# Two causal convolutions: reading the products from PSUM instead of from SBUF copies

## The chip, the cores and the metric

One core of a Trainium2 chip runs the whole program. The time is the device time of one execution in microseconds (us); the number compared is the median of several executions of the same kernel. TensorE (PE) does the matmuls and writes into PSUM, a small memory of banks; VectorE (DVE), ScalarE (ACT) and GpSimd (POOL) do the elementwise work; SyncE (SP) issues most DMA transfers between HBM and SBUF.

## The reference

One step of a hybrid decoder layer over 2048 prompt rows and 8 sequences of 8 sample rows, 1024 columns wide, all in float32. A projection of the normalised rows feeds three mixers (gated delta rule, S5, HGRN2); their outputs are concatenated and projected back; then comes a channel mixer with a convolution, and a gated embedding. Two places hold a causal convolution of each column over time, with 4 taps for q, k and v and with 3 taps for the up projection:

```
def causal_dwconv(x, buf, w):
    xp = jnp.concatenate([buf.astype(x.dtype), x], axis=1)
    y = xp[:, 0:t] * w[0]
    for j in range(1, width):
        y = y + xp[:, j:j + t] * w[j]
    return y, xp[:, t:]
...
z = rmsnorm(h, norm_mix[i]) @ w_in[i]
qkv, buf_qkv = causal_dwconv(z_qkv, conv_qkv[i], dn_conv_w[i])
...
h = h + jnp.concatenate([o_a, o_b, o_c], axis=-1) @ w_out[i]
up, buf_ffn = causal_dwconv(rmsnorm(h, norm_ffn[i]) @ ffn_w_up[i], conv_ffn[i], ffn_conv_w[i])
a_ff, b_ff = jnp.split(up, 2, axis=-1)
h = h + (jax.nn.silu(a_ff) * b_ff) @ ffn_w_down[i]
```

The prompt starts with zero rows before it; each of the 8 sample sequences starts with given state rows (`state_conv_qkv`, `state_conv_ffn`). The last rows before the end are outputs too.

## The kernel before

The rows are cut into four groups of 512; the last has the 64 sample rows with it. The matmuls are float32 products in three passes (high by high, low by high, high by low part), so a unit of 128 output columns by up to 512 rows takes 24 matmuls into one of three PSUM banks named `mm`. Stages follow one another: phase 1 (input projection, to about 900 us), the first output projection for groups 0 and 1 (phase 3, about 900 to 1090), their up projection (phase 4, to 1784), the second output projection for groups 2 and 3 (1784 to 1891), their up projection (to 2416), the down projection (phase 5, to 2934), and the end (phase 6). All that is the foreground; its matmuls are called `mm`.

Beside it runs the background: generators for the three mixers, for norms and for setup, whose matmuls go into PSUM banks named `mx`. Each chunk of the delta rule needs a triangular inverse, made four times in the program by 31 pairs of TENSOR_TENSOR `R<-Q,R` and TENSOR_REDUCE `R<-R` on VectorE. HGRN2 goes group by group, each in two halves: loads into `hw`, levels that multiply and merge (`mx<-hw`), the merged tile `mx<-ident,hw`, four rounds on the state `SH`, a norm, a transpose `mx<-ident,b`, and a store to `oT`.

The order of everything is decided while the program is built. `Pace` (L44) keeps for each engine the time at which a cost model sees it free, from every instruction issued, its operands and the rings of its tiles. After each foreground matmul `tick` (L740) runs evacuations that are due (`later`, L754: when the model sees the tile ready, or after so many ticks at the latest) and then lets background generators take steps whose inputs the model sees ready. `need` (L749) is the exception: where the foreground cannot go on without a flag, it runs the background alone, forced, until the flag is set. On the chip each engine then simply takes its instructions in that order. All instructions are issued from one helper, `call` at L71, so rows of the profile are told apart by their tiles.

A convolution unit goes like this. `conv_evac` (L885) lets ACT copy the product from its bank into an SBUF tile `raw` with room for the rows before it, and write the last tap, `y = w * product`; the bank is then free. `edges` fills the rows before (on POOL, from `tail`, `ftail`, `stq` or `fst`), `conv` (L894) adds the other taps on VectorE with SCALAR_TENSOR_TENSOR `y<-raw,w,y`, and `keep` lets POOL save the last rows. The ring `raw` has two tiles of 603 columns. It has two other users: `ffn_state` (L2255) loads the 11 blocks of 16 state rows of the second convolution into it (`fs_rows`), transposes them on TensorE and copies them to `fst`; and in the first output projection every fourth pair of residual tiles stands in it (`pair`, L2184). Other residual pairs are `h1x` tiles of the ring `nx` (four tiles of 1024 columns, shared with the norms) or `y` tiles.

Of the kernel before, what the change touches and what calls it, by code (L numbers as in the profile page):

```python
# [9 lines left out]
F32 = mybir.dt.float32  # L10
# [4 lines left out]
OP = mybir.AluOpType  # L15
# [431 lines left out]
class Model:  # L447
# [420 lines left out]
    def edges(self, raw, taps, first, tail, rows):  # L868


        nc = self.nc
        k = taps - 1
        if first:
            nc.gpsimd.memset(raw[:, 0:k], 0.0)
        else:
            nc.gpsimd.tensor_copy(raw[:, 0:k], tail)
        if rows is not None:
            nc.gpsimd.tensor_copy(self.sample_part(raw, taps)[:, :, 0:k], rows)

    @staticmethod  # L880
    def sample_part(raw, taps):
        k = taps - 1
        return raw[:, k + 512:k + 512 + NSEQ * (k + ST)].rearrange("p (s t) -> p s t", t=k + ST)

    def conv_evac(self, raw, y, ps, c1, m, taps, w):  # L885

        k = taps - 1
# [6 lines left out]
    def conv(self, y, raw, w, taps, n):  # L894

        for j in range(taps - 1):
            self.nc.vector.scalar_tensor_tensor(y[:, :512], raw[:, j:j + 512], w[:, j:j + 1], y[:, :512], op0=OP.mult,
                                                op1=OP.add)
        if n > 512:
            ys, rs = y[:, 512:].rearrange("p (s t) -> p s t", t=8), self.sample_part(raw, taps)  # L900
            for j in range(taps - 1):
                self.nc.vector.scalar_tensor_tensor(ys, rs[:, :, j:j + 8], w[:, j:j + 1], ys, op0=OP.mult, op1=OP.add)

    def keep(self, raw, taps, last, tail, out):

        nc = self.nc
        k = taps - 1
        if last:
            nc.gpsimd.tensor_copy(out[:, 0:k], raw[:, 512:512 + k])
            nc.gpsimd.tensor_copy(out[:, k:].rearrange("p (s t) -> p s t", t=k), self.sample_part(raw, taps)[:, :, 8:])  # L910
        else:
            nc.gpsimd.tensor_copy(tail, raw[:, 512:512 + k])

    def p1_evac(self, g, kind, b, c1, m, ps):
        nc = self.nc
        n = self.group(g)[1]
        if c1 == 0:
            self.y = self.cv.tile([128, 512 + NS], F32, tag="y", name="y", bufs=3)
            if kind == "qkv":
                self.raw = self.cv.tile([128, 3 + 512 + NSEQ * 11], F32, tag="raw", name="raw")  # L920
                self.edges(self.raw, 4, g == 0, self.tail[:, b],
                           self.stq[:, b].rearrange("p (s t) -> p s t", t=3) if g == 3 else None)
        y = self.y
        if kind == "qkv":
            self.conv_evac(self.raw, y, ps, c1, m, 4, self.cw[:, b])
# [14 lines left out]
    def p1_finish(self, g, kind, b, y):  # L940
# [15 lines left out]
        def conv(raw=self.raw if kind == "qkv" else None):  # L956
            self.conv(y, raw, self.cw[:, b], 4, n)
            self.keep(raw, 4, g == 3, self.tail[:, b], self.cso[:, b])
            self.later(y, silu, 9)

# [10 lines left out]
        if kind == "qkv":  # L971
            self.later(self.raw, conv, 12)
        else:
            self.later(y, bound if kind == "hf" else out, 12)
# [1198 lines left out]
    def phase3(self, units, wo, between, direct):  # L2173
# [4 lines left out]
        half_tile = lambda tag, w, bufs: self.cv.tile([128, w], F32, tag=tag, name="xh", bufs=bufs)[:, :512]  # L2178
        y_tile = lambda: half_tile("y", 512 + NS, 3)
# [675 lines left out]
```

## Time and profile before

| | |
|---|---|
| median of 3 runs | 3197.21 us (3195.34 to 3198.12) |
| the profiled execution | 3197.67 us, its span 3195.9 us |
| mean granted TensorE clock | 0.981 of full speed |
| TensorE busy | 3059.7 us, 96% of the span |
| VectorE, ScalarE, GpSimd busy | 1882.4, 1196.0 and 899.9 us |

A share of busy time is an average over all stages. A row of a timeline gives the start, the duration, the engine and the instruction, and in brackets how long its engine had stood idle before it and what released it. Tile numbers are left out, so `mm` is any of the three product banks.

### The profile page before, as it was taken

The numbers are of one execution on the slowest core, as the hardware profiler recorded it, in microseconds if no ns is written. First come the engines' busy times: TensorE is split into PE (matmuls) and PEld (weight loads), VectorE is DVE, ScalarE is ACT, GpSimd is POOL, SyncE is SP. The second block draws the span as 40 slices with busy tenths as digits, with TensorE's granted clock in tenths as the row PEclk, the third lists the DMA queues.
The fourth block names the chain that finished last, engine by engine and source line by source line (L and its number), as shares of the span: only waits on it lengthen the run. The fifth ranks groups of instructions, "written<-read, shape, count | busy, mean of one in ns | idle before, by whom it ended". The sixth has DMA issues, their size and how long they took to land.

```text
span 3195.9 us, 49480 instructions
## 1 busy us (share of the span) xinstructions
PE 3059.7 (96%) x17872; PEld 2541.0 (80%) x17872; DVE 1882.4 (59%) x4195; ACT 1196.0 (37%) x2823; POOL 899.9 (28%) x1316
## 2 busy tenths in 40 slices
PE   6999999999987999999999999999999999999998
PEld 5778788888876776777777788998998888888886
DVE  8864587893665678955656446455454323223665
ACT  4354344344333543324334234333333213222333
POOL 3352234222424332234434215333331000000111
PEclk8999999999988999999999999999999999999999
DMA  6245654367655443554224333222216445444221
GB/s 181 86 136 168 183 139 144 108 175 209 194 148 160 135 144 102 147 159 133 79 72 120 118 107 116 68 68 71 65 51 190 131 124 169 132 131 128 79 85 57
DMA packets 576845, 400.31 MB, mean 125 GB/s; under 512 B 111078, under 2 KB 503146, under 8 KB 576329
## 3 DMA queue, kind: packets, MB, share of 16 engines
q1 hardware_dynamic: 545656, 359.07, 39.1%
q10 hardware_dynamic: 30944, 38.09, 3.5%
q8 instruction: 141, 2.31, 0.3%
q14 instruction: 104, 0.84, 0.1%
HBM read 277.52 MB, written 118.95 MB: 124 GB/s over the span
## 4 chain that ended last, share of the span: by engine, by line
PE 57%; DVE 3%; DMA 1%; issue 1%; ACT 1%; SPq 1%; POOL 0%; DVEq 0%; ACTq 0%; POOLq 0%
PE mm L71 51%; PE mx L71 6%; DVE y L71 1%; SPq L71 1%; DVE R L71 1%; DVE b L71 0%; DVE s5v L71 0%; DVE rs L71 0%; POOL wl L71 0%; DMA b<-xs 0%; DMA kr<-gT 0%; DMA wr<-in_ffn_w_up 0%; DMA fs_rows<-in_state_conv_ffn 0%; ACT b L71 0%; ACT raw L71 0%
## 5 line engine op out<-in xcount | busy, mean ns | idle before, releaser
L71 PE MATMUL mm<-hnh,wh 128*128 128x512 f32 (+2 forms) x2720 | 980.1, 360 | 9.7 <-ACT y L71 9.7
L71 PE MATMUL mm<-hnl,wh 128*128 128x512 f32 (+2 forms) x2720 | 982.3, 361 | 4.1 <-DVE hnl L71 4.1
L71 PE MATMUL mm<-hnh,wl 128*128 128x512 f32 (+2 forms) x2720 | 980.2, 360 | 0.0
L71 DVE SCALAR_TENSOR_TENSOR y<-raw,fw,y 128x512 f32<-128x512 f32 (+1 forms) x440 | 408.6, 937 | 372.9 <-ACT y L71 324.0
L71 PEld LDWEIGHTS mm<-hnh,wh 128*128 128x128 f32 x2720 | 516.7, 190 | 85.1 <-ACT y L71 11.0
L71 PEld LDWEIGHTS mm<-hnl,wh 128*128 128x128 f32 x2720 | 516.2, 190 | 78.7 <-issue 4.8
L71 PEld LDWEIGHTS mm<-hnh,wl 128*128 128x128 f32 x2720 | 516.6, 190 | 73.7 <-issue 4.7
L71 POOL TENSOR_TENSOR wl<-wr,wh 128x512 fp32r<-128x512 f32 (+1 forms) x303 | 429.4, 1428 | 476.3 <-ACT wh L71 463.5
L71 ACT ACTIVATE raw<-mm 128x512 f32<-128x512 f32 (+3 forms) x336 | 155.3, 462 | 383.1 <-PE mm L71 365.5
L71 PE MATMUL mm<-kh,ghi 128*128 128x512 f32 x748 | 295.0, 394 | 0.8 <-ACT kh L71 0.8
L71 PE MATMUL mm<-kl,ghi 128*128 128x512 f32 x748 | 294.4, 394 | 0.3 <-DVE kl L71 0.2
L71 PE MATMUL mm<-kh,glo 128*128 128x512 f32 x704 | 277.1, 394 | 0.0
L71 ACT ACTIVATE wh<-wr 128x512 fp32r<-128x512 f32 (+1 forms) x338 | 204.9, 633 | 139.4 <-PE mm L71 61.7
L71 ACT ACTIVATE y<-y 128x512 f32<-128x512 f32 (+1 forms) x136 | 87.7, 645 | 363.4 <-DVE y L71 359.0
L71 ACT ACTIVATE ghi<-kr 128x512 fp32r<-128x512 f32 (+1 forms) x192 | 99.0, 580 | 332.0 <-PE mm L71 280.0
L71 DVE TENSOR_TENSOR h<-mm,h 128x512 f32<-128x512 f32 (+1 forms) x36 | 24.8, 690 | 281.3 <-PE mm L71 281.2
L71 DVE SCALAR_TENSOR_TENSOR y<-raw,cw,y 128x512 f32<-128x512 f32 (+1 forms) x180 | 153.5, 858 | 40.0 <-ACT y L71 22.5
L71 PEld LDWEIGHTS mm<-kh,ghi 128*128 128x128 f32 x748 | 140.6, 188 | 33.3 <-ACT kh L71 1.2
L71 PEld LDWEIGHTS mm<-kl,ghi 128*128 128x128 f32 x748 | 140.6, 188 | 33.2 <-DVE kl L71 1.5
L71 PEld LDWEIGHTS mm<-kh,glo 128*128 128x128 f32 x704 | 132.2, 188 | 29.9 <-DVE glo L71 0.4
L71 POOL COPY ftail<-raw 128x2 f32<-128x2 f32 x132 | 29.3, 222 | 442.1 <-ACT raw L71 441.9
L71 ACT ACTIVATE y<-mm,fw 128x512 f32<-128x512 f32 (+2 forms) x220 | 133.7, 608 | 5.6 <-DVE y L71 5.0
(525 smaller groups left out, 4664.4 us busy)
## 6 DMA issues: line engine op xcount, KB each, us to landing
wr<-in_ffn_w_up SPq DMA_DIRECT2D x176, 256.0 KB
kr<-gT SPq DMA_DIRECT2D x155, 256.0 KB
wr<-in_w_in SPq DMA_DIRECT2D x112, 256.0 KB
gT<-y SPq DMA_DIRECT2D x66, 256.0 KB
h<-h SPq DMA_DIRECT2D x65, 256.0 KB
Q<-zq SPq DMA_DIRECT2D x32, 512.0 KB
wr<-oT SPq DMA_DIRECT2D x48, 256.0 KB
kr<-in_ffn_w_down SPq DMA_DIRECT2D x44, 256.0 KB
```

Of the source, the lines that this page charges most:

```text
L71: return f(*a, **k)
```

## The change

The product stays in its PSUM bank until the convolution is done. ACT writes the last tap into `y` as before, and copies only the last 2 or 3 columns into a small tile (`tail`, `ftail`, `ct`, or the output tiles). VectorE adds the other taps from the bank; the first columns, which need rows from before the block, are added by separate small instructions from that tile or from the state rows. Group 3's two blocks, which were convolved together once both had been copied, are now convolved one by one. `edges`, `conv` and `keep` go with the ring `raw`; `fs_rows` and the fourth residual pair go into the ring `nx`. In the diff `...` marks cuts.

```diff
     def conv_evac(...)
-        self.copy_act(raw[:, k + c1:k + c1 + mp], ps[:, :mp])
         self.copy_act(y[:, c1:c1 + m], ps[:, :m], w[:, k:k + 1])
+        self.copy_act(out[:, 0:k], ps[:, mp - k:mp])
         if mp < m:
-            self.copy_act(self.sample_part(raw, taps)[:, :, k:], ps[:, mp:m].rearrange("p (s t) -> p s t", t=8))
+            self.copy_act(out[:, k:].rearrange("p (s t) -> p s t", t=k), self.by_seq(ps[:, mp:m])[:, :, ST - k:])
+
+        def add(o, i, j):
+            nc.vector.scalar_tensor_tensor(o, i, w[:, j:j + 1], o, op0=OP.mult, op1=OP.add)
+
+        def conv():
+            for j in range(k):
+                add(y[:, c1 + k - j:c1 + mp], ps[:, :mp - k + j], j)
+            if mp < m:
+                ys, xs = self.by_seq(y[:, 512:512 + NS]), self.by_seq(ps[:, mp:m])
+                for j in range(k):
+                    add(ys[:, :, k - j:], xs[:, :, :ST - k + j], j)
+                for j in range(k):
+                    add(ys[:, :, :k - j], rows[:, :, j:], j)
+            if tail is not None:
+                for j in range(k):
+                    add(y[:, c1:c1 + k - j], tail[:, j:k], j)
+
+        return conv
+
+    def conv_block(self, y, ps, c1, m, n, taps, w, g, tail, rows, out):
+        last = c1 + m == n
+        if c1 == 0:
+            self.before = None if g == 0 else tail[:, (g - 1) % 2]
+        to = (out if g == 3 else tail[:, g % 2]) if last else self.sm.tile([128, 3], F32, tag="ct", name="ct")
+        conv = self.conv_evac(y, ps, c1, m, taps, w, self.before, rows, last, to)
+        self.before = to
+        return conv
...
     def p1_evac(...)
+            def rest():
+                conv()
+                if c1 + m == n:
+                    self.p1_finish(g, kind, b, y)
+            self.later(y, rest, 9)
...
     def pair(i):
             t = i % 8 % turn
-            if t < 2:
+            if t != 2:
                 return halves(self.np_.tile([128, DM], F32, tag="nx", name="h1x", bufs=self.NX))
-            if t == 2:
-                self.h1y = i
-            return tuple(y_tile() if t == 2 else half_tile("raw", 3 + 512 + NSEQ * 11, 2) for _ in range(2))
+            self.h1y = i
+            return y_tile(), y_tile()
...
     def ffn_state(self):
-            sr = self.cv.tile([128, 3 + 512 + NSEQ * 11], F32, tag="raw", name="fs_rows")[:16, :512]
+            sr = self.np_.tile([128, DM], F32, tag="nx", name="fs_rows", bufs=self.NX)[:16, :512]
...
     def p4_evac(...)
         def conv():
-            self.conv(y, raw, self.fw[:, b], 3, n)
-            self.keep(raw, 3, g == 3, self.ftail[:, b], self.fso[:, b] if g == 3 else None)
+            block()
+            if c1 + m < n:
+                return
...
-        if c1 + m == n:
-            self.later(raw, conv, 9)
+        self.later(y, conv, 6)
```

Since the planner sees other instructions and other rings, the order of the rest moves too. The order of the changed kernel holds the same 12368 `mm` and 2911 `mx` matmuls; VectorE's instructions grow from 4197 to 4935, POOL's fall from 1321 to 767. Three places follow.

TensorE in the first output projection of before, ahead of unit 4: `ident,b` is the transpose that ends the first half of HGRN group 1, `uf`, `pp` and `d_g` belong to chunks of the delta rule, `woh`, `wol` to foreground matmuls.

```order
L71 MATMUL mx<-ident,b_9699 128x128 x4
L71 MATMUL mm<-wol,wh 128x512
L71 MATMUL mx<-uf_2060,pp 32x32 x8
L71 MATMUL mx<-pp,uf_2060 32x32 x4
L71 MATMUL mm<-woh,wl 128x512
...
L71 MATMUL mx<-d_g,le_785 64x4
L71 MATMUL mx<-d_g,blk 64x4
L71 MATMUL mx<-gb,ones 128x32
L71 MATMUL mx<-t_9751,NN 64x64 x4
```

The same place of the changed kernel, from the last foreground matmul ahead of unit 4 on (the 288 matmuls that follow it are `mx`).

```order
L71 MATMUL mm<-woh,wl 128x512
L71 MATMUL mx<-ident,hw 128x128 x4
L71 MATMUL mx<-b_9151,b_9638 128x128 x2
...
L71 MATMUL mx<-ident,V 128x128 x4
L71 MATMUL mx<-ident,b_9781 128x128 x4
L71 MATMUL mx<-hw 64x96 x16
L71 MATMUL mx<-hw 64x32 x48
L71 MATMUL mx<-hw 48x32 x16
L71 MATMUL mx<-hw 32x32 x16
```

In before the first half ends between foreground matmuls and the run without them begins with chunk work; now the end of the first half and all levels of the second lie in the run.

VectorE at the third inverse, before: `R<-Q,R` is its first step, `hw` and `b` are levels of HGRN's first half of group 1.

```order
L71 TENSOR_TENSOR b_8751<-mx,id_892 128x256 x2
L71 TENSOR_TENSOR hw<-hw 128x256
L71 COPY_PREDICATED b_8751<-hm,mx 128x128 x2
L71 TENSOR_TENSOR hw<-hw,b_8752 128x128x2
L71 COPY_PREDICATED b_8751<-hm,mx 128x64x2 x2
L71 TENSOR_TENSOR R_8994<-Q,R_8993 128x2
L71 TENSOR_REDUCE R_8993<-R_8994 128x1
```

And after, where `hw` and `b` are levels of the second half (between the cuts stand the rest of the 31 pairs and nothing else).

```order
L71 TENSOR_TENSOR b_9887<-mx,id_881 128x256 x2
L71 TENSOR_TENSOR hw<-hw 128x256
L71 COPY_PREDICATED b_9887<-hm,mx 128x128 x2
L71 TENSOR_TENSOR R_9916<-Q,R_9915 128x2
L71 TENSOR_REDUCE R_9915<-R_9916 128x1
...
L71 TENSOR_TENSOR R_9916<-Q,R_9915 128x512
L71 TENSOR_REDUCE R_9915<-R_9916 128x16
L71 TENSOR_TENSOR hw<-hw,b_9888 128x128x2
L71 COPY_PREDICATED b_9887<-hm,mx 128x64x2 x2
```

The inverse moved from the first half's levels, in phase 1, to the second half's, in the run ahead of unit 4.

SyncE's loads in the second output projection, before (`wr` are rows of the mixers' output for the next units, `gT` stores, `h1x` residual rows).

```order
L71 DMA fs_rows_17904<-in_state_conv_ffn 16x512
L71 DMA fs_rows_17944<-in_state_conv_ffn 16x512
L71 DMA wr_17947<-oT_79 128x4x128
L71 DMA wr_17955<-oT_79 128x4x128
L71 DMA gT_81<-y_17911 128x512
L71 DMA h1x_17976<-in_x_prompt 128x512 x2
L71 DMA fs_rows_17985<-in_state_conv_ffn 16x512
L71 DMA wr_18004<-oT_79 128x4x128
L71 DMA wr_18012<-oT_79 128x4x128
```

And after.

```order
L71 DMA wr_17951<-oT_79 128x4x128
L71 DMA fs_rows_17980<-in_state_conv_ffn 16x512
L71 DMA fs_rows_17994<-in_state_conv_ffn 16x512
L71 DMA fs_rows_18002<-in_state_conv_ffn 16x512
L71 DMA fs_rows_18010<-in_state_conv_ffn 16x512
L71 DMA fs_rows_18018<-in_state_conv_ffn 16x512
L71 DMA fs_rows_18026<-in_state_conv_ffn 16x512
L71 DMA fs_rows_18034<-in_state_conv_ffn 16x512
L71 DMA fs_rows_18042<-in_state_conv_ffn 16x512
L71 DMA h1x_18109<-in_x_prompt 128x512
```

Eight of the eleven loads moved together; on TensorE their eight transposes also follow one another, and then those of three `h1x` tiles, with no `mm` between.

## Rows read from the trace of the kernel before

**Rows 1.** The page: busy time of each engine, the chain by line, and groups.

```profile
PE 3059.7 (96%) x17872; PEld 2541.0 (80%) x17872; DVE 1882.4 (59%) x4195; ACT 1196.0 (37%) x2823; POOL 899.9 (28%) x1316
...
PE mm L71 51%; PE mx L71 6%; DVE y L71 1%; SPq L71 1%; DVE R L71 1%; DVE b L71 0%; DVE s5v L71 0%; DVE rs L71 0%; POOL wl L71 0%; DMA b<-xs 0%; DMA kr<-gT 0%; DMA wr<-in_ffn_w_up 0%; DMA fs_rows<-in_state_conv_ffn 0%; ACT b L71 0%; ACT raw L71 0%
...
L71 DVE SCALAR_TENSOR_TENSOR y<-raw,fw,y 128x512 f32<-128x512 f32 (+1 forms) x440 | 408.6, 937 | 372.9 <-ACT y L71 324.0
...
L71 DVE SCALAR_TENSOR_TENSOR y<-raw,cw,y 128x512 f32<-128x512 f32 (+1 forms) x180 | 153.5, 858 | 40.0 <-ACT y L71 22.5
...
L71 ACT ACTIVATE raw<-mm 128x512 f32<-128x512 f32 (+3 forms) x336 | 155.3, 462 | 383.1 <-PE mm L71 365.5
```

**Rows 2.** Windows: per stage, busy us (instructions) of PE, PEld, DVE, ACT, POOL; clock; DMA.

```profile
928.00:1004.00 76.00, 53.63 (x611) 46.39 (x612) 43.72 (x155) 20.66 (x93) 13.06 (x19) 0.74 0.41 112
...
1784.00:1891.00 107.00, 104.98 (x490) 84.82 (x490) 50.98 (x127) 30.84 (x66) 21.61 (x19) 1.00 0.40 129
...
1891.00:2416.00 525.00, 523.68 (x3182) 475.55 (x3181) 275.51 (x332) 204.31 (x455) 196.26 (x349) 1.00 0.23 72
```

**Rows 3.** Timeline, 928 to 1004: start, duration, engine, instructions, [idle before <- releaser].

```profile
928.78 0.74 DVE L71 SCALAR_TENSOR_TENSOR hw<-mx,ghg,hw 128x512 f32<-128x512 f32 x1
...
935.37 0.62 POOL L71 COPY hw<-hw 128x512 f32<-128x512 f32 x1 [13.70 <-DMA hw<-hq]
...
943.10 0.89 PE L71 MATMUL mx<-hw 64*64 64x96 f32 x32 [1.84 <-POOL hw L71]
...
967.12 0.80 PE L71 MATMUL mx<-ident,hw 128*128 128x128 f32 x4
...
996.63 1.11 PE L71 MATMUL mx<-ident,b 128*128 128x128 f32 x4 [7.08 <-POOL b L71]
...
1003.01 0.63 ACT L71 ACTIVATE wh<-wr 128x512 fp32r<-128x512 f32 x1 [9.83 <-DMA wr<-oT]
```

**Rows 4.** Lines by shape, DVE: count | busy us, mean ns | idle before.

```profile
L71 DVE SCALAR_TENSOR_TENSOR y<-raw,fw,y 128x512 f32<-128x512 f32 x352 | 344.9, 980 | 371.3 <-ACT y L71 324.0 <-POOL ftail L71 24.4 <-POOL raw L71 12.2
...
L71 DVE SCALAR_TENSOR_TENSOR ZG<-mx,gdn,ZG 128x512 f32<-128x512 f32 x16 | 12.0, 747 | 3.2 <-PE mx L71 3.1
...
L71 DVE SCALAR_TENSOR_TENSOR SH<-SH,b,mx 64x64 f32<-64x64 f32 x128 | 35.8, 279 | 18.5 <-PE mx L71 15.2 <-POOL raw L71 0.4
...
L71 DVE SCALAR_TENSOR_TENSOR rs<-rs 128x1 f32<-128x1 f32 x320 | 70.1, 219 | 11.2
```

**Rows 5.** Lines by shape, ACT and POOL, the same columns.

```profile
L71 ACT ACTIVATE raw<-mm 128x64 f32<-128x64 f32 x56 | 13.0, 232 | 0.0
...
L71 POOL COPY raw<-ftail 128x2 f32<-128x2 f32 x132 | 32.0, 243 | 6.0 <-PE mx L71 4.5 <-DVE y L71 1.5
```

**Rows 6.** Timeline, DVE, the third inverse's first instruction.

```profile
846.16 0.16 DVE L71 TENSOR_TENSOR R<-Q,R 128x2 f32<-128x2 f32 x1 [1.19 <-POOL R L71]
```

**Rows 7.** Lines, DVE, the four triangular inverses together.

```profile
L71 DVE TENSOR_TENSOR R<-Q,R 128x2 f32<-128x2 f32 (+30 forms) x124 | 75.6, 610 | 9.3 <-POOL R L71 5.6
...
L71 DVE TENSOR_REDUCE R<-R 128x1 f32<-128x2 f32 (+30 forms) x124 | 43.4, 350 | 4.3
```

**Rows 8.** Timeline, 1791 to 1810: loads and transposes of fs_rows, and the norm behind them.

```profile
1791.86 0.36 SPq L71 DMA_DIRECT2D fs_rows<-in_state_conv_ffn  x1
...
1793.84 0.43 SPq L71 DMA_DIRECT2D fs_rows<-in_state_conv_ffn  x1
...
1795.08 0.39 PE L71 MATMUL mx<-ident,fs_rows 16*128 16x16 f32 x4 [0.81 <-DMA fs_rows<-in_state_conv_ffn]
...
1798.94 0.39 PE L71 MATMUL mx<-ident,fs_rows 16*128 16x16 f32 x4 [0.71 <-DMA fs_rows<-in_state_conv_ffn]
...
1806.90 0.23 DVE L71 COPY fst<-mx 128x64 f32<-128x64 f32 x1 [1.99 <-PE mx L71]
...
1808.95 1.41 DVE L71 SCALAR_TENSOR_TENSOR h1x<-h1x,nrs,g_ffn 128x512 f32<-128x512 f32 x2
```

**Rows 9.** Waits, PE, 60 to 900: us in total, times, longest.

```profile
PE mm L71 <- ACT y L71: 8.4, 4, 4.1
```

More of the change, by code (lines that the diff above doesn't have):

```diff
@@ L866, in p1_unit, with by_seq, conv_evac @@
             self.later(ps, lambda a=(g, kind, b, c1, m, ps): self.p1_evac(*a), 6)
-    def edges(self, raw, taps, first, tail, rows):
+    @staticmethod
+    def by_seq(ap):
+        return ap.rearrange("p (s t) -> p s t", t=ST)
+    def conv_evac(self, y, ps, c1, m, taps, w, tail, rows, last, out):
         nc = self.nc
         k = taps - 1
[L873 to L878, printed above, removed]
@@ L894, in conv @@
[L894 to L902, printed above, removed]
@@ L904, in keep @@
[L904 to L912, printed above, removed]
+            self.copy_act(out[:, k:].rearrange("p (s t) -> p s t", t=k), self.by_seq(ps[:, mp:m])[:, :, ST - k:])
+        def add(o, i, j):
+            nc.vector.scalar_tensor_tensor(o, i, w[:, j:j + 1], o, op0=OP.mult, op1=OP.add)
@@ L918, in p1_evac @@
             self.y = self.cv.tile([128, 512 + NS], F32, tag="y", name="y", bufs=3)
[L919 to L922, printed above, removed]
         y = self.y
         if kind == "qkv":
-            self.conv_evac(self.raw, y, ps, c1, m, 4, self.cw[:, b])
+            conv = self.conv_block(y, ps, c1, m, n, 4, self.cw[:, b], g, self.tail[:, b],
+                                   self.stq[:, b].rearrange("p (s t) -> p s t", t=3), self.cso[:, b])
+            def rest():
[4 more added lines that the diff above has]
+            return
         elif kind == "u":
@@ L954, in out @@
             self.flags.add((kind, b, g))
[L956 to L959, printed above, removed]
         def silu():
@@ L971, in p1_finish @@
         if kind == "qkv":
-            self.later(self.raw, conv, 12)
+            self.later(y, silu, 9)
         else:
@@ L2177, in phase3 @@
         both = units[0][0] == units[1][0]
[L2178 to L2179 removed]
+        y_tile = lambda: self.cv.tile([128, 512 + NS], F32, tag="y", name="xh", bufs=3)[:, :512]
         turn = 3 if both else 4
@@ L2238, in ffn_consts @@
         self.fw = cp.tile([128, 44, 3], F32, name="fw")
-        self.ftail = cp.tile([128, 44, 2], F32, name="ftail")
+        self.ftail = cp.tile([128, 44, 2, 2], F32, name="ftail")
     def ffn_setup(self):
@@ L2322, in p4_evac @@
                 self.need(("hn2", self.h1y))
-            self.raw = self.cv.tile([128, 3 + 512 + NSEQ * 11], F32, tag="raw", name="raw")
             self.y = self.cv.tile([128, 512 + NS], F32, tag="y", name="y", bufs=3)
-            self.edges(self.raw, 3, g == 0, self.ftail[:, b],
-                       self.fst[:, b].rearrange("p (s t) -> p s t", t=2) if g == 3 else None)
-        raw, y = self.raw, self.y
-        self.conv_evac(raw, y, ps, c1, m, 3, self.fw[:, b])
+        y = self.y
+        block = self.conv_block(y, ps, c1, m, n, 3, self.fw[:, b], g, self.ftail[:, b],
+                                self.fst[:, b].rearrange("p (s t) -> p s t", t=2) if g == 3 else None,
+                                self.fso[:, b] if g == 3 else None)
         def conv():
-            self.conv(y, raw, self.fw[:, b], 3, n)
-            self.keep(raw, 3, g == 3, self.ftail[:, b], self.fso[:, b] if g == 3 else None)
+            block()
+            if c1 + m < n:
+                return
             if x == 0:
@@ L2586, in setup_small @@
         self.stq = cp.tile([128, 12, 24], F32, name="stq")
-        self.tail = cp.tile([128, 12, 3], F32, name="tail")
+        self.tail = cp.tile([128, 12, 2, 3], F32, name="tail")
         self.cso = self.cp.tile([128, 12, 27], F32, name="cso")
```

6 lines of the change are left out of this document (removed).

## The prediction

> **What bounds the kernel now.** I read the page's busy times first: TensorE works 3059.7 of 3195.9 us, and the chain that ended last lies on it almost throughout [rows 1]. So the question is not how much work the other engines have but where TensorE stands still: about 136 us in all. The windows by stage show where. From 1891 to 2416 us, in the middle of the second half of the up projection with its convolutions, TensorE is busy 523.7 of 525 us: no relief of another engine is worth anything there. The largest hole is 928 to 1004 us, 53.6 us busy out of 76, and those at a granted clock of 0.74; the second output projection, 1784 to 1891, loses only 2 us [rows 2]. The remaining 112 us are smaller holes elsewhere.
>
> The hole at 928 has a plain cause. Unit 4 of the first output projection needs the HGRN output of group 1, and `need` runs the background alone until it is there: no foreground matmul is issued meanwhile. The timeline shows a chain from engine to engine: the last result of the half before at 928.78, the load of the next half until 935.37, the levels from 943.10, the merged tile at 967.12, four rounds with their norm until the transpose at 996.63, and the cast of the reloaded rows at 1003.01, which foreground matmuls follow [rows 3]. I call that the forced stretch.
>
> **The convolutions themselves: no gain in sum.** What they cost on VectorE now is 408.6 + 153.5 = 562 us [rows 1]. A 512-column step takes 980 ns from SBUF, while a step of the same kind with an operand in PSUM takes 747 [rows 4]. Afterwards the order holds 372 steps of nearly 512 columns, 124 of nearly 320, 124 of nearly 192, 124 of 64, 124 of 8 sequences' first rows, and 496 of one to three columns. At 747 ns the first are 278 us. The middle sizes stand in no row: between 279 ns (64 columns [rows 4]) and 747; by columns I take 0.50 and 0.35, that is 62 and 43 us. The 64-column ones and the first rows at 279 are 35 us each, the 496 slivers at 219 ns [rows 4] are 109. Sum 562, bounds 512 (both middle sizes at 279) and 642 (both at 747). What the shorter reads give, the extra pieces take.
>
> What goes beside it: 336 copies into `raw` on ACT go, 155 us [rows 1], and 336 small copies come in at up to the 232 ns of a 64-column one [rows 5], 78 us. On POOL some 550 instructions go, mostly copies like the 243 ns one [rows 5], about 130 us. Both engines are busy only 37% and 28% [rows 1], so this saves TensorE nothing directly.
>
> Two inputs from SBUF cost 980 ns, one 747 [rows 4]; no row says why. The Trainium skill, "SBUF — State Buffer", section "Who interferes with whom", says that a VectorE instruction with two SBUF inputs contends with a GpSimd instruction that reads SBUF and that one with a single SBUF input does not; the two rows agree with it, and by that rule POOL's steps beside the convolutions would shorten too. The fast rival below has this mechanism.
>
> **Term 1: the forced stretch gets longer, +40 us.** The planner inside the kernel (a cost model evaluated while the program is built) sees a different VectorE and other rings and therefore places background work later: at the start of the first output projection 1129 background matmuls stand ahead instead of 1327. What is left is caught up where the foreground must wait. In the order of before, the first half of HGRN group 1 and the third triangular inverse stand ahead of the run that unit 4 forces; now the run begins with that first half's merged tile, holds the whole second half, and on VectorE the 31 instruction pairs of the inverse stand between the second half's first and second level, so every later level queues behind them. Before, the inverse began at 846.16 us [rows 6], beside foreground matmuls.
>
> Piece by piece, from the rows of before:
> - first half, merged tile to last transpose: 967.12 to 996.63 plus 1.1 = 30.6 us [rows 3].
> - store, loads, first level: 928.78 to 943.10 = 14.3 us, of which the loads end at 935.37 (6.6 us) and the rest waited partly behind chunk work on VectorE, which is not there now. I take 9.
> - the inverse: (75.6 + 43.4) / 4 = 29.8 us, up to 33.2 with a quarter of the idle time (9.3 + 4.3) before its steps [rows 7].
> - the other levels: 943.10 to 967.12 = 24 us with chunk chains between; I take 15.
> - merged tile to the first foreground cast: 967.12 to 1003.01 = 35.9 us.
>
> In before three chunk chains of the delta rule run between these steps, now fewer, so apart from the inverse each row's span is an upper bound; as a lower one I take its half, an estimate. Sum 120, bounds 82 (52.4 + 29.8) and 138, against 74.2 us (928.78 to 1003.01). That is +46. Against it stands work that TensorE now does inside the stretch instead of beside foreground matmuls: 288 background matmuls in the run instead of 315, but larger ones (the chunks' 128-wide Grams come in, 32-wide solves go out). I credit 6 us. Net +40, near the rows' own spans since the engines' hand-overs stay; bounds +2 (82 with the credit) and +64 (138 without). What is late next is only the same reloaded tile, so nothing hides it.
>
> **Term 2: the state rows of the second convolution, +20 us.** The eleven `fs_rows` loads lose the `raw` ring and share the ring of four normalised-row tiles with `h1x`. In before their transposes lie singly between foreground matmuls and TensorE waits for two of them, 0.81 and 0.71 us [rows 8]. Now two of four tiles hold `h1x` rows that wait for their norm, and eight loads stand in one run on SyncE, their eight transposes in one run on TensorE, with no foreground matmul between them, because unit 11's `need` asks for the norm behind them. With two tiles in turn the run is three round trips after the first pair. A round trip is 1791.86 to 1795.08 = 3.2 us or 1793.84 to 1798.94 = 5.1 [rows 8]; at 4.5 with the release that is 13.5, the first pair's rest 2.5. The norm chain stands behind the last copy of state rows on VectorE: 1806.90 to the end of 1808.95 + 1.41 is 3.5 us [rows 8], and it comes twice, 7 us. Sum 23, less the 2 us that TensorE waits there now and 1 for work done meanwhile: +20. Bounds: 9 (trips of 3.2, the second norm hidden, the first pair there in time) and 27 (trips of 5.1, nothing hidden).
>
> **Term 3: everything else, -4 us.** A product bank is now held until VectorE has convolved from it, where ACT's copy freed it before. Three banks rotate, so a late VectorE stops TensorE: before 900 us TensorE already waits for ACT's `y` copies 8.4 us in four places [rows 9], the place where such a wait would grow. Bounds: -28, a quarter of the 112 us of smaller holes, since 198 background matmuls fewer stand before 900 us and VectorE's single steps are shorter; and +20, if waits like those four (2.1 us each) come at ten units. I take -4, the middle, because nothing in the rows picks a side. The Trainium skill, "PSUM — Partial Sum Buffer", section "Summary: rules for kernel authors", asks to evacuate PSUM promptly, which speaks against reading it two or three times from there; by it the sum would be that of the rival on banks below; no row of before shows a bank held that long.
>
> **Sum.** The profiled execution took 3197.67 us (0.46 above the median 3197.21 of the three runs). 3197.7 + 40 + 20 - 4 = 3253.7, that is 1.8% slower.
>
> **Rivals.**
> - *Faster by less contention.* The holes before 900 us and around 1000 to 1400 shrink since VectorE's steps no longer meet POOL's, and the run at unit 4 is shorter than its pieces because nothing else loads the engines. For it: 980 against 747 ns. Against it: TensorE is full from 1891 on, and both runs stand in the order. It needs the stretch near its low bound (+10), the state rows at +9, and 45 of the 112 us of smaller holes gone: 3197.7 + 10 + 9 - 45 = 3172.
> - *Only one of the two runs costs.* If the state rows land early, or if the forced stretch's chains overlap, one term remains: 3197.7 + 20 to 3197.7 + 40 less 4, about 3214 to 3234; I take 3220.
> - *All hidden.* TensorE at 96% absorbs both (their background work is done anyway and would otherwise cost elsewhere): 3197.
> - *The banks decide.* VectorE falls behind in phase 1 and in each unit of the up projections TensorE waits for a bank: from the point where VectorE lies more than two units behind, each such unit costs the rest of its steps. Adding +20 to +45 to the two terms gives 3278 to 3303; I take 3290. For it: 4 waits of up to 4.1 us for `y` [rows 9]; against it: in window 1891 to 2416 VectorE is busy only 275.5 of 525 us [rows 2].
>
> **How the numbers follow.** Forecast (both runs cost, banks do not) 0.60, one run only 0.17, banks 0.09, faster 0.09, hidden 0.05. The range reaches into the one-run case and most of the bank case: 3207 to 3290. No change means within 0.2% (6.4 us), about what a measurement of this kernel can tell: faster 0.10, same 0.05, slower 0.85.
>
> **What would show it.** Right: in the profile after, a hole of some 120 us near 900 to 1030 us with the `R<-Q,R` and `R<-R` pairs of one inverse in the middle and no `mm` matmul; TensorE idle about 20 us in the second output projection, ended by DMA `fs_rows` and by DVE `h1x`; `y<-mm,fw,y` at about 750 ns; POOL and ACT shorter by about 130 and 77 us with no effect. Wrong: the inverse's pairs lie beside foreground matmuls; `fs_rows` waits of under 5 us in sum; or long waits "PE mm <- DVE y", which would mean banks. The forecast fails as a whole if TensorE's idle time in the profile after is not about 55 us above 136.

## The result and the profile after

The changed kernel is slower: 3271.97 us median (3268.46 to 3281.92, 4 runs) against 3197.66 us (3195.34 to 3199.16, 4 runs) for the kernel before; the ratio is 1.0237, 95% interval 1.0223 to 1.025. The forecast of 3254 lies 18 us below it, the range 3207 to 3290 holds it. The profiled execution has a span of 3266.9 us, 71.0 more than before.

The page of the changed kernel, busy times and the chain by line, against [rows 1]:

```profile
PE 3067.0 (94%) x17872; PEld 2549.7 (78%) x17872; DVE 1953.8 (60%) x4933; ACT 1091.2 (33%) x2820; POOL 726.5 (22%) x762
...
PE mm L71 48%; PE mx L71 6%; DVE y L71 2%; DVE R L71 1%; DVE b L71 1%; DVE s5v L71 0%; DMA Q<-dNN 0%; POOL wl L71 0%; DMA fs_rows<-in_state_conv_ffn 0%; DVE s5t L71 0%; DMA kr<-in_ffn_w_down 0%; DMA kr<-gT 0%; DVE rs L71 0%; ACT b L71 0%; DVE kl L71 0%
```

TensorE is as busy as before (7.3 us more) and stands still 199.9 us instead of 136.2. ACT lost 105 us of work, POOL 173, and VectorE gained 71. To see where the time went, I counted foreground matmuls in both traces (each holds all 12368) and took the time from the start of one to the start of another, the same two in both, and how long TensorE stood idle in between:

| foreground matmuls | stage | before, us | after, us | difference | idle before | idle after |
|---|---|---|---|---|---|---|
| to 3288 | phase 1 | 898.0 | 866.2 | -31.8 | 68.4 | 71.7 |
| 3288 to 3380 | first output projection, ahead of unit 4 | 27.7 | 52.3 | +24.5 | 2.5 | 15.4 |
| 3380 to 3395 | the forced stretch | 83.0 | 123.9 | +40.9 | 22.4 | 60.7 |
| 3395 to 5784 | its rest and the first up projection | 775.6 | 801.5 | +25.9 | 28.1 | 31.7 |
| 5784 to 5960 | second output projection, its middle | 46.5 | 59.4 | +12.9 | 2.0 | 8.8 |
| from 5960 | all the rest | 1365.0 | 1363.7 | -1.4 | 12.8 | 11.6 |

The same work stands in other places: phase 1 is shorter since some 200 background matmuls left it, and what follows is longer by more. In sum TensorE has next to nothing more to do; the idle columns show what was lost, most of it ahead of unit 4 (12.9 us) and in the forced stretch (38.3 us). From the middle of the second output projection on nothing got longer, although the up projection of groups 2 and 3 with its convolutions lies there. The windows by stage, against [rows 2] (stretch, PE, PEld, DVE, ACT, POOL, clock, DMA):

```profile
914.60:1041.90 127.30, 66.62 (x614) 52.06 (x613) 76.74 (x258) 27.24 (x121) 17.39 (x29) 0.64 0.38 102
1842.20:1962.00 119.80, 111.03 (x518) 89.41 (x517) 53.27 (x137) 31.87 (x69) 25.05 (x20) 0.94 0.37 119
1962.00:2488.20 526.20, 524.93 (x3185) 476.61 (x3184) 329.66 (x766) 164.63 (x455) 115.57 (x90) 1.00 0.23 72
```

In the last of them VectorE is busy 330 us instead of 276 and POOL 116 instead of 196, and TensorE still works 524.9 of 526.2 us. The forced stretch, in the timeline of the changed kernel, against [rows 3]:

```profile
921.18 0.63 PE L71 MATMUL mx<-ident,hw 128*128 128x128 f32 x4 [0.90 <-DVE A L71]
...
948.61 0.74 DVE L71 SCALAR_TENSOR_TENSOR hw<-mx,ghg,hw 128x512 f32<-128x512 f32 x1
...
957.22 1.56 PE L71 MATMUL mx<-hw 64*64 64x96 f32 x32 [14.17 <-POOL hw L71]
...
964.28 0.16 DVE L71 TENSOR_TENSOR R<-Q,R 128x2 f32<-128x2 f32 x1 [3.60 <-POOL R L71]
...
991.56 0.69 DVE L71 TENSOR_REDUCE R<-R 128x16 f32<-128x512 f32 x1
...
992.73 1.08 PE L71 MATMUL mx<-hw 64*64 64x32 f32 x32 [31.51 <-DVE hw L71]
...
1001.00 1.12 PE L71 MATMUL mx<-ident,hw 128*128 128x128 f32 x4 [1.11 <-POOL hw L71]
...
1035.63 0.63 ACT L71 ACTIVATE wh<-wr 128x512 fp32r<-128x512 f32 x1 [1.51 <-DMA wr<-oT]
```

Read the brackets: at 992.73 TensorE had stood 31.51 us, and VectorE's `hw` step that released it stood behind the last step of the inverse at 991.56. In [rows 3] no wait of TensorE is over 7.1 us.

The convolution's steps on VectorE in the changed kernel, by line (count | busy us, mean ns | idle before), against the two lines of 408.6 and 153.5 us in [rows 1]:

```profile
L71 DVE SCALAR_TENSOR_TENSOR y<-mm,fw,y 128x510 f32<-128x510 f32 (+7 forms) x528 | 302.0, 579 | 273.6 <-ACT ftail L71 189.6 <-ACT ct L71 40.4 <-ACT fso L71 33.3
L71 DVE SCALAR_TENSOR_TENSOR y<-mm,cw,y 128x511 f32<-128x511 f32 (+8 forms) x216 | 123.8, 578 | 38.6 <-ACT tail L71 20.6 <-ACT ct L71 12.5
L71 DVE SCALAR_TENSOR_TENSOR y<-ftail,fw,y 128x2 f32<-128x2 f32 (+1 forms) x264 | 90.3, 342 | 9.3
L71 DVE SCALAR_TENSOR_TENSOR y<-fst,fw,y 128x16 f32<-128x16 f32 x88 | 55.9, 635 | 3.1
L71 DVE SCALAR_TENSOR_TENSOR y<-tail,cw,y 128x3 f32<-128x3 f32 (+2 forms) x108 | 34.8, 323 | 3.8
L71 DVE SCALAR_TENSOR_TENSOR y<-ct,fw,y 128x2 f32<-128x2 f32 x88 | 21.1, 240 | 1.6
L71 DVE SCALAR_TENSOR_TENSOR y<-stq,cw,y 128x24 f32<-128x24 f32 (+2 forms) x36 | 11.5, 319 | 1.3
L71 DVE SCALAR_TENSOR_TENSOR y<-ct,cw,y 128x3 f32<-128x3 f32 (+2 forms) x36 | 9.8, 272 | 0.8
```

The reads from PSUM are cheap, 426 us in all. But the 496 steps of one to three columns (`ftail`, `tail`, `ct`) cost 156 us, 315 ns each, and the 124 on state rows 67 us. The sum is 649 us, 87 more than before.

The second output projection, timeline of the changed kernel, against [rows 8]:

```profile
1878.33 1.02 PE L71 MATMUL mx<-ident,fs_rows 16*128 16x16 f32 x8 [1.46 <-DMA fs_rows<-in_state_conv_ffn]
1880.73 1.05 PE L71 MATMUL mx<-ident,fs_rows 16*128 16x16 f32 x8 [1.38 <-DMA fs_rows<-in_state_conv_ffn]
...
1881.82 0.23 DVE L71 COPY fst<-mx 128x64 f32<-128x64 f32 x1 [0.25 <-PE mx L71]
...
1884.76 1.94 PE L71 MATMUL mx<-ident,h1x 128*128 128x128 f32 x8 [2.98 <-DVE h1x L71]
...
1888.00 1.09 PE L71 MATMUL mx<-ident,h1x 128*128 128x128 f32 x4 [1.30 <-DVE h1x L71]
```

The run of state rows and norms is there as forecast, with a pair of transposes every 2.4 us (eight matmuls are two sets of state rows). From foreground matmul 5904 to 5905 it leaves a gap of 14.9 us, where before has 0.9.

### The profile page after: what moved, and what is told of

Same layout as the page of the kernel before. It is cut to its first block, busy times and chain, and to the rows that moved or that the text cites. A ratio compares the mean times of both kernels' runs of the same rounds, so it can differ in the third digit from the quotient of the medians.

```text
span 3266.9 us, 49568 instructions
## 1 busy us (share of the span) xinstructions
PE 3067.0 (94%) x17872; PEld 2549.7 (78%) x17872; DVE 1953.8 (60%) x4933; ACT 1091.2 (33%) x2820; POOL 726.5 (22%) x762
## 4 chain that ended last, share of the span: by engine, by line
PE 54%; DVE 4%; issue 1%; DMA 1%; ACT 1%; POOL 0%; SPq 0%; DVEq 0%; ACTq 0%; POOLq 0%
PE mm L71 48%; PE mx L71 6%; DVE y L71 2%; DVE R L71 1%; DVE b L71 1%; DVE s5v L71 0%; DMA Q<-dNN 0%; POOL wl L71 0%; DMA fs_rows<-in_state_conv_ffn 0%; DVE s5t L71 0%; DMA kr<-in_ffn_w_down 0%; DMA kr<-gT 0%; DVE rs L71 0%; ACT b L71 0%; DVE kl L71 0%
## 5 line engine op out<-in xcount | busy, mean ns | idle before, releaser
L71 PE MATMUL mm<-hnh,wh 128*128 128x512 f32 (+2 forms) x2720 | 982.7, 361 | 22.8 <-DVE y L71 12.9
L71 POOL TENSOR_TENSOR wl<-wr,wh 128x512 fp32r<-128x512 f32 (+1 forms) x309 | 409.4, 1338 | 1218.8 <-ACT wh L71 1162.7
L71 DVE SCALAR_TENSOR_TENSOR y<-mm,fw,y 128x510 f32<-128x510 f32 (+7 forms) x528 | 302.0, 579 | 273.6 <-ACT ftail L71 189.6
L71 PEld LDWEIGHTS mm<-kl,ghi 128*128 128x128 f32 x748 | 140.6, 188 | 31.7
L71 DVE SCALAR_TENSOR_TENSOR y<-mm,cw,y 128x511 f32<-128x511 f32 (+8 forms) x216 | 123.8, 578 | 38.6 <-ACT tail L71 20.6
L71 POOL TENSOR_TENSOR kl<-kr,kh 128x512 fp32r<-128x512 f32 x13 | 18.3, 1409 | 472.7 <-ACT kh L71 464.4
L71 PE MATMUL mx<-b,b 64*64 64x64 f32 (+7 forms) x752 | 105.6, 287 | 14.3 <-DMA b<-us 11.4
```

Source lines behind the costliest of these rows:

```text
L71: return f(*a, **k)
```

## The experiments

My theory went through two forms. The first: the planner's order is the whole cause, and reading from PSUM costs nothing in sum. Its rivals: banks held until VectorE has read them; and the shared ring in the second output projection. The first four runs test them. They share one chip, where the kernel before took 3203.63 us (7 runs); the ratios are against it.

**e1_plan_blind.** One edit in the cost model, in which the small steps read as nothing:

```diff
     def dve(self, op, outs, ins):
+        if op == "scalar_tensor_tensor" and ins[0].tensor.name.rsplit("_", 1)[0] in ("tail", "ftail", "ct", "cso", "fst", "stq"):
+            return 0.0
```

> The changed kernel with one edit in the planner's cost model: the small VectorE steps of the convolutions (those that read tail, ftail, ct, cso, fst or stq) count as nothing when the order is made; the instructions stay the same. In its order 1331 background matmuls stand ahead of the first output projection (1125 in the changed kernel, 1327 before), the run at unit 4 holds 203 background matmuls and only the last 3 of the 31 steps of the inverse, and no run of state rows stands in the second output projection. Theory (the plan is the cause, reading from PSUM costs nothing in sum): about 3197 us, between 3185 and 3210. Rival (PSUM reads and banks held are the cause): 3240 us or more, since every convolution still reads PSUM. Rival (less contention pays once the plan is right): 3170 to 3185.

Measured: 3249.8 us, ratio 1.0147 (1.0125 to 1.0169). A miss. The forced stretch did shrink, to 63.6 us by the count of matmuls (83.0 before, 123.9 in the changed kernel), but phase 1 now takes 916.6 us, 19 more than before, and the trace's waits of TensorE show a new first row (us, times, longest); in the changed kernel it is 12.9 us, in the kernel before it is not listed:

```profile
PE mm L71 <- DVE y L71: 31.4, 13, 6.1
```

The expectation was also wrong on the order: the trace still has a run of state rows, 28 of their 44 transposes between foreground matmuls 5904 and 5905, and the middle of the second output projection takes 65.1 us. So the first theory is half of it: with the inverse out of the forced stretch, TensorE waits for banks that VectorE has not yet read. Whether that is because banks are held, or because VectorE has more to do, this run can't tell.

**e2_inverse_later.** While an operand is forced, the generator of the chunks' inverse is skipped:

```diff
             else:
+                self.m.bg.skip = self.m.dgen
                 assert self.m.bg.tick(4, True), "an operand that never comes"
+                self.m.bg.skip = None
...
+            if gen is self.skip:
+                continue
```

> The changed kernel, but while unit 4's operand is forced, the generator that holds the triangular inverse is skipped: the inverse goes to foreground matmuls 3807 to 3969, the run at unit 4 shrinks from 288 to 176 background matmuls, and the run of state rows in the second output projection is gone from the order too. Theory: the stretch loses the 31.5 us that TensorE waits for the inverse and the chunk preparation, the second output projection its 13 us, and some of it comes back later: 3228 us, between 3218 and 3245. Rival (PSUM reads and banks): 3260 us or more.

Measured: 3243.25 us, ratio 1.0133 (1.011 to 1.0157), inside the expected range. The stretch falls from 123.9 to 84.1 us, about as long as before. But 3395 to 5784 rises from 801.5 to 825.9: more than half of it is given back, since the inverse's chunks come later.

**e3_state_ring.** `fs_rows` in a ring of their own:

```diff
-            sr = self.np_.tile([128, DM], F32, tag="nx", name="fs_rows", bufs=self.NX)[:16, :512]
+            sr = self.cv.tile([128, 512], F32, tag="fsr", name="fs_rows", bufs=2)[:16]
```

> The changed kernel with fs_rows in a ring of their own, two tiles of 512 columns. Up to the second output projection the order is that of the changed kernel (run of 288 at unit 4 with the inverse); the run of state rows at foreground matmul 5904 is gone. Theory: the 13 us that the second output projection became longer come back and nothing else: 3259 us, between 3254 and 3264. Rival (that stage is longer for another reason): 3268 to 3275.

Measured: 3280.3 us, ratio 1.0245 (1.0222 to 1.0268): no gain. The middle of the second output projection takes 60.2 us (59.4 in the changed kernel), with the waits of its TensorE in 1860 to 1930 nearly what they were:

```profile
PE mx L71 <- DVE h1x L71: 4.3, 2, 3.0
PE mx L71 <- DMA fs_rows<-in_state_conv_ffn: 4.2, 4, 1.5
```

What was expected of the order did not come: the trace has 28 of the 44 transposes of state rows in one run behind foreground matmul 5904 (32 in the changed kernel). So this run does not test a projection without the run of state rows; it shows that a ring of their own does not take the run away. What the traces show instead is a late start: the generator of the state rows is started when the background is empty, and its first transposes stand behind foreground matmul 5662 before, 5852 in both the changed kernel and this run. Its last loads and the norms behind them are then forced. Over all kernels of this document the length of this stretch goes with that run: 42.5 to 46.5 us in the five without one (before, e5, e7, e8, e10), 53.7 us with 8 transposes in it (e2), 57.5 with 16 (e4), 59.4 to 65.1 with 28 or 32 (the changed kernel, e1, e3, e6, e9).

**e4_before_plan.** The kernel before, only its plan changed:

```diff
     def dve(self, op, outs, ins):
+        if op == "scalar_tensor_tensor" and ins[0].tensor.name.rsplit("_", 1)[0] == "raw":
+            return 0.10 + 0.125 + self.size(outs[0]) / 960
```

> The kernel before, its convolutions from SBUF copies as they were; only the planner counts each convolution step on VectorE 0.10 us dearer. In its order the third inverse now stands whole in the run at unit 4, which has 207 background matmuls (315 before), and 1283 stand ahead of the first output projection. Theory (the place of the inverse is the cause, not the convolution): the run gets longer by the inverse's 31 us less the chunk chains that leave it: 3212 us, between 3204 and 3232. Rival (PSUM reads are the cause): 3197 us, since nothing in the convolutions changed.

Measured: 3235.51 us, ratio 1.0108 (1.0079 to 1.0136), above the upper end of what I expected. The same instructions as before, in another order: the stretch takes 100.8 us (83.0 before), and in the trace's waits of TensorE from 950 to 1060 us stands

```profile
PE mx L71 <- DVE hw L71: 28.6, 1, 28.6
```

No convolution reads PSUM here, so an order with the inverse in that place costs without the change. Not all of the loss is the inverse: of 37.2 us between the two profiled executions 17.8 lie in the stretch, 15.3 in matmuls 3395 to 5784 and 11.0 in the second output projection, whose state rows also come late (16 transposes in a run); phase 1 is 5.7 shorter. The expectation counted the stretch alone.

The second form of the theory: what costs is VectorE's added work (A), paid either through the order, when the planner sees it, or in waits, when it doesn't; against that, banks held (B). The next four runs were made for these two; the kernel before took 3199.5 us there (21 runs).

**e5_before_load.** The kernel before in its own order, with small steps added that the planner does not see (`self.nc.nc` is the real engine):

```diff
+    def conv(self, y, raw, w, taps, n, g=0):
+        for j in range((taps - 1) * (g > 0)):
+            o = self.dm[:, :taps - 1 - j]
+            self.nc.nc.vector.scalar_tensor_tensor(o, raw[:, j:taps - 1], w[:, j:j + 1], o, op0=OP.mult, op1=OP.add)
```

> The kernel before, in its own order, convolutions from SBUF; VectorE gets 372 small steps more (scratch columns, 1 to 3 wide, beside the convolutions of groups 1 to 3), which the planner does not see. At 0.22 to 0.37 us each (what the changed kernel's one- and two-column steps took) that is 82 to 138 us more work for VectorE, near the 88 us by which the changed kernel's convolution steps grew. No bank is held longer. Theory A (the added VectorE work is what costs, TensorE waits for late VectorE): 3215 to 3245 us. Theory B (PSUM banks held by the convolution are what costs): 3197 to 3208.

Measured: 3216.99 us, ratio 1.0054 (1.0042 to 1.0067). The added steps, lines of VectorE:

```profile
L898 DVE SCALAR_TENSOR_TENSOR dm<-raw,fw,dm 128x2 f32<-128x2 f32 (+1 forms) x264 | 72.3, 274 | 35.7 <-POOL raw L71 30.9
L898 DVE SCALAR_TENSOR_TENSOR dm<-raw,cw,dm 128x3 f32<-128x3 f32 (+2 forms) x108 | 36.7, 340 | 2.7
```

109 us of steps off TensorE's path cost 17 us, at the low end of A's range. By the count of matmuls 12.0 us of it fall in phase 1 (910.0 us against 898.0).

**e6_no_slivers.** e1 in the same order, with the planner told of the small steps but the steps not issued:

```diff
                 for j in range(k):
-                    add(y[:, c1:c1 + k - j], tail[:, j:k], j)
+                    o = y[:, c1:c1 + k - j]
+                    nc.note(nc.vector, "scalar_tensor_tensor", (o, tail[:, j:k], w[:, j:j + 1], o), {})
```

> The kernel of e1_plan_blind in the same order, without the 496 one- to three-column steps that add the rows before a block, so the first columns of each block lack their older taps. Banks are still held until VectorE has read them. Theory A (VectorE's added work): e1's time less most of its 46 us, 3205 to 3228 us. Theory B (banks held): 3240 to 3250, as e1.

Measured: 3200.48 us, ratio 1.0005 (0.9995 to 1.0016). This is the run that decides: same order, same banks, same PSUM reads, and the whole 1.4% of e1 is gone. By the count of matmuls 30.2 of the 45.8 us between the two profiled executions come back in phase 1 (886.4 us against 916.6). It went further than A expected. B falls as a cause by itself. Whether held banks make late VectorE work dearer is not shown: the steps cost 46 us for 159 us of work here and 17 us for 109 in e5, where no bank is held, but the two orders differ. The row "PE mm <- DVE y" goes from 31.4 to 18.4 us: a bank is waited for when VectorE is late.

**e7_slivers_pool.** The small steps on GpSimd, planner blind to them:

```diff
+                tmp = self.sm.tile([128, 3], F32, tag="cp", name="cp")
                 for j in range(k):
-                    add(y[:, c1:c1 + k - j], tail[:, j:k], j)
+                    o = y[:, c1:c1 + k - j]
+                    nc.gpsimd.tensor_mul(tmp[:, :k - j], tail[:, j:k], w[:, j:j + 1].to_broadcast([128, k - j]))
+                    nc.gpsimd.tensor_add(o, o, tmp[:, :k - j])
```

> The changed kernel with the 496 one- to three-column steps moved from VectorE to GpSimd, each as a multiply and an add, and with neither counted by the planner, as in e1_plan_blind. Its order is near e1's (1311 background matmuls ahead of the first output projection, 287 in the run at unit 4, of the inverse only the last 3 steps). Theory A: VectorE is relieved of some 140 us, 3210 to 3235 us. Theory B (banks): 3240 to 3255; if GpSimd's steps are waited for, more.

Measured: 3223.88 us, ratio 1.0076 (1.0062 to 1.009), in A's range, half of e1's loss. It is not a clean test of the engine, since the order is another: 287 background matmuls in the run at unit 4 (203 in e1), and no run of state rows in the second output projection (42.8 us against 65.1).

**e8_before_ring.** The kernel before with the new `pair` and `ffn_state`, as in the diff of the change.

> The kernel before with only its ring changed: fs_rows and the fourth residual pair use the ring of normalised rows as in the changed kernel, the convolutions still read SBUF copies. The state rows are loaded from foreground matmul 5634 on, as before, and their transposes lie singly. Theory (the second output projection became longer because the background ends later, not because of the ring): no change, 3195 to 3204 us. Rival (the shared ring costs): 3206 to 3220.

Measured: 3197.76 us, ratio 0.9989 (0.9978 to 1.0). The shared ring costs nothing: with it, and an early start, the middle of the second output projection takes 42.5 us.

Two more, with the kernel before at 3198.36 us (15 runs).

**e9_order_kept.** The edit of e6 on the changed kernel itself, whose order stays.

> The changed kernel in its own order, without the 496 one- to three-column steps that add the rows before a block, so the first columns of each block lack their older taps; the planner still counts them. The run at unit 4 still has 288 background matmuls and the whole inverse. Theory (two ways of paying: the order that the planner made is a cost by itself): 3235 to 3258 us, since the run ahead of unit 4 stays some 40 us longer and the second output projection some 10. Rival (only VectorE's executed load costs): 3200 to 3215.

Measured: 3255.72 us, ratio 1.0174 (1.0153 to 1.0195). Of the changed kernel's 2.37% the order alone keeps 1.74; executing the steps is the other 0.63. That split depends on which is taken out first. Without the small steps, e1's order stands at 1.0005 (e6) and the changed kernel's at 1.0174 (e9); with them, at 1.0147 (e1) and 1.0237. So the steps cost 1.42% of before's time in one order and 0.63% in the other, the order 1.69% without the steps and 0.90% with them: the two losses overlap. In e9's waits of TensorE two of the changed kernel's stand as they were, the one for the inverse and one for `d_g`:

```profile
PE mx L71 <- DVE hw L71: 32.3, 2, 31.7
...
PE mx L71 <- DVE d_g L71: 18.3, 2, 13.6
```

**e10_carry.** The convolution from PSUM with one small step per block. GpSimd multiplies and adds the last columns ahead of time; VectorE adds the result:

```diff
+            pool.tensor_mul(cc[:, :k], to[:, :k], w[:, 0:1].to_broadcast([128, k]))
+            for j in range(1, k):
+                tmp = self.sm.tile([128, 3], F32, tag="cp", name="cp")
+                pool.tensor_mul(tmp[:, :k - j], to[:, j:k], w[:, j:j + 1].to_broadcast([128, k - j]))
+                pool.tensor_add(cc[:, :k - j], cc[:, :k - j], tmp[:, :k - j])
...
-                for j in range(k):
-                    add(y[:, c1:c1 + k - j], tail[:, j:k], j)
+                nc.vector.tensor_add(y[:, c1:c1 + k], y[:, c1:c1 + k], tail[:, :k])
```

> The changed kernel with the rows before a block prepared on GpSimd: as soon as the last columns are copied, GpSimd multiplies them with the taps and adds them up, and the next block needs one add of 2 or 3 columns on VectorE, 124 instead of 496 small steps. The planner counts these as nothing. In its order 1347 background matmuls stand ahead of the first output projection and the run at unit 4 has 136 with no step of the inverse. Theory A: near e6, 3190 to 3212 us; below 3191 it would beat the kernel before. Rival (any step between a bank and y costs): 3225 or more.

Measured: 3205.5 us, ratio 1.0018 (1.0005 to 1.003), within A. The small steps on VectorE (`ftail`, `tail`, and `cc` for a second block) are 224, not the 124 that were expected, and take 62 us:

```profile
L71 DVE TENSOR_TENSOR y<-y,ftail 128x2 f32<-128x2 f32 x132 | 35.1, 266 | 8.0
L71 DVE TENSOR_TENSOR y<-y,tail 128x3 f32<-128x3 f32 x36 | 17.2, 478 | 1.8
L71 DVE TENSOR_TENSOR y<-y,cc 128x2 f32<-128x2 f32 (+1 forms) x56 | 9.7, 173 | 0.0
```

The convolution from PSUM can be had for nearly nothing, and gives nothing: TensorE was not waiting for what it saves. No run pointed to a version that beats the kernel before.

## Why the prediction was right, and where it was not

**The bound and the direction.** Right. TensorE's idle time rose by 63.7 us, where I had asked for about 55. Two signs came out otherwise. TensorE's waits for `fs_rows` are 4.5 us in sum, and under 5 I had called wrong; in the second output projection it is idle 8.8 us (119.80 less 111.03) where I asked for about 20. POOL and ACT fell by more than forecast, 173 and 105 us, with no effect. Of the waits "PE mm <- DVE y" that would have meant banks, there are seven, 12.9 us in sum, the longest 3.8.

**Term 1, +40: measured +40.9** between matmuls 3380 and 3395. The pieces: first half 28.2 us (921.18 to the end of 948.61; I took 30.6), store to first level 8.6 (9), the inverse as TensorE's wait 31.5 (29.8), the other levels 12.3 (43.8 from 957.22 to 1001.00 less 31.5; 15), merged tile to cast 34.6 (35.9): 115 in sum, against 120. Less the 74.2 us of before that is 41 without the 6 us that I credited for work done meanwhile: pieces 5 us too long and a credit that did not show cancelled, so the closeness is partly luck. e2 and e4 show the inverse in that place as the cause, one by taking it out, one by putting it in.

**Term 2, +20: measured +12.9, and its cause was wrong.** The run and the double norm are there, but e3 and e8 show that the shared ring does not make it: with a ring of their own the state rows still stand in a run, and with the shared one and an early start they don't. It is the late end of the background, which puts their first transposes 190 foreground matmuls later. And a trip is short: 2.4 us for a pair (1878.33 to 1880.73), where I took 4.5 us. The bounds don't follow from their own terms either: these give about 10 and 23 to 25, not 9 and 27.

**The sum of the convolutions: the step that failed.** "No gain in sum" (562 us; its terms give bounds of 525, not 512, and 642) measured 649, above the upper bound. The steps that read PSUM came out near what was worked out, 426 us against 418. The 496 small ones cost 315 ns each where I took 219, and the 124 on state rows 544 where I took 279. That alone is 80 of the 87 us. The trace shows what was missing: I compared each step's span with those of GpSimd's instructions. 379 of the 496 ran while GpSimd did nothing, at 220 ns, the price I took; the other 117 overlapped a GpSimd instruction and took 622 ns on average. Of the 124 it is 62 at 237 ns and 62 at 850. At the undisturbed prices the sum would be 564. So the price of a small step was right; what was left out is that GpSimd works beside a quarter of the 496 and half of the 124.

The premise of the large steps reads differently too. Of before's 352 steps of 512 columns, the 980 ns, 155 ran with GpSimd idle, at 751 ns, and 197 overlapped it, at 1160. From PSUM the 511-column step takes 750 ns in both cases (87 and 45 steps). So in these steps reading PSUM is no faster; what goes is the price of overlapping GpSimd. The change freed the large steps of it and exposed hundreds of small ones to it.

And I let this work stand as costless because TensorE bounds the kernel; e5 (17 us for 109) and e6 (all of e1's loss) show that it is not costless before 1800 us, where the mixers' chains and the convolution share VectorE.

**Term 3, -4: measured +17.2** (71.0 less 40.9 and 12.9). Moved work gives most of the shifts in time, -31.8 in phase 1, +24.5 ahead of unit 4, +25.9 later, -1.4 at the end, but in sum it is even: TensorE's idle time in these four stretches grew by 18.6 us, so all of the term is new standing still. 12.9 of it lies ahead of unit 4, and nearly all of that is one wait of 13.6 us for `d_g` between the last matmul of phase 1 and the first of the output projection (below), which comes again in e9. I had no row for it.

**The rivals.** Less contention did not pay, though its mechanism is there (980 to 750 ns): POOL's and ACT's work fell by 278 us together, and with the order and the small steps set right (e6, e10) the time is that of before. That banks decide fell in e6, as a cause by itself. The Trainium skill's request to evacuate PSUM promptly ("PSUM — Partial Sum Buffer", "Summary: rules for kernel authors") thus did not bind here as long as VectorE was on time.

**Still open.** Why the lag of the planner takes just this order, that is which of its queues passes which, was not taken apart: e4 shows only that 0.10 us on each convolution step suffices to move the inverse. Whether held banks make late VectorE work dearer was not settled either.

## What to carry to other kernels

Where a planner in the kernel makes the order, price an edit twice: what its instructions take on the chip, and where the planner then puts everything else; look first for what it moves into a stretch in which the bounding engine has nothing else to do. When a copy is replaced by reads at the edge of a block, count the edge pieces, not the bytes: hundreds of steps of two columns on VectorE cost more than what was saved on engines that nobody waited for. Take a step's price with and without GpSimd at work beside it, and count how often each will happen. Work removed from engines that nobody waited for gave nothing here, though it was 278 us.

## What the runs showed of the hardware

A VectorE step with two SBUF inputs takes longer when it overlaps a GpSimd instruction. In the timeline of the changed kernel (start, us), the two small steps of a block, first with GpSimd idle, then beside it:

```profile
2008.22 0.47 DVE L71 SCALAR_TENSOR_TENSOR y<-ftail,fw,y 128x2 f32<-128x2 f32 x2
...
2009.13 1.45 POOL L71 TENSOR_TENSOR kl<-kr,kh 128x512 fp32r<-128x512 f32 x1 [4.59 <-ACT kh L71]
...
2010.50 1.60 DVE L71 SCALAR_TENSOR_TENSOR y<-ftail,fw,y 128x2 f32<-128x2 f32 x2
...
2010.54 1.29 POOL L71 TENSOR_TENSOR wl<-wr,wh 128x512 fp32r<-128x512 f32 x1
```

The wait of 13.6 us has such steps ahead of it:

```profile
870.92 4.65 POOL L71 TENSOR_TENSOR wol<-wor,woh 128x1024 fp32r<-128x1024 f32 x2 [2.67 <-ACT woh L71]
...
871.06 8.39 DVE L71 SCALAR_TENSOR_TENSOR dsc<-dsc 128x16 f32<-128x16 f32 x8
...
880.01 0.61 PE L71 MATMUL mx<-d_g,le 128*128 128x16 f32 x2 [13.57 <-DVE d_g L71]
```

That is 1.05 us for a step of 16 columns (8.39 / 8). Of the 40 steps of that line and shape in the trace, 29 ran with GpSimd idle, at 174 to 176 ns; the other 11 had a mean of 964 ns, the longest 2271. The Trainium skill, "SBUF — State Buffer", "Who interferes with whom", says that a VectorE instruction with two SBUF inputs contends with a GpSimd instruction that reads SBUF; these counts agree. No run took GpSimd's work away; the comparison is between steps of one trace.

Steps that read PSUM do not show this (511 columns: 749 to 752 ns beside GpSimd, 748 to 751 without). By shape, in the changed kernel:

```profile
L71 DVE SCALAR_TENSOR_TENSOR y<-mm,fw,y 128x511 f32<-128x511 f32 x132 | 99.0, 750 | 4.7
...
L71 DVE SCALAR_TENSOR_TENSOR y<-mm,fw,y 128x191 f32<-128x191 f32 x44 | 18.4, 417 | 1.5
...
L71 DVE SCALAR_TENSOR_TENSOR y<-mm,fw,y 128x56 f32<-128x56 f32 x44 | 12.1, 276 | 1.6
```

From the first and the last, a column costs 1.04 ns ((750 - 276) / 455) and a step 0.22 us ahead of its columns (276 - 56 x 1.04 = 218 ns); the same line gives 417 for 191 columns, where 417 were measured. The undisturbed 220 ns of a step of one to three columns are that fixed part.
